# SwiGLU by seven block products in place of eight, in a two-layer decoder trunk

## The chip, the cores and the metric

One NeuronCore of a Trainium2 chip runs the whole program. Its engines are TensorE (matmuls and transposes, written PE in the profile, with weight loads as PEld), VectorE (DVE), ScalarE (ACT), GpSimd (POOL) and SyncE (SP, which here only issues transfers). The metric is the time of one execution on the device in microseconds, lower is better. Profile times below are counted from the start of the profiled span.

## The reference: what is computed

Two layers over 512 tokens of width 1024, in float32:

```python
for layer in range(2):
    x = x + 0.5 * swiglu(rmsnorm(x, ffn1_norm[layer]), ffn1_w_gate_up[layer], ffn1_w_down[layer])
    x = x + hybrid_mixer(rmsnorm(x, mix_norm[layer]), ...)     # 8 forgetting heads, 4 differential heads
    x = x + 0.5 * swiglu(rmsnorm(x, ffn2_norm[layer]), ffn2_w_gate_up[layer], ffn2_w_down[layer])
return rmsnorm(x, final_norm)

def swiglu(h, w_gate_up, w_down):                              # 1024 -> 2 x 2816 -> 1024
    g, u = split(h @ w_gate_up, 2)
    return (silu(g) * u) @ w_down
```

So there are four SwiGLU blocks and two mixers. The change concerns the SwiGLU blocks and the form in which x is kept between all of them.

## The kernel before, in words

Each float32 operand of a matmul is split into two parts of the engine's reduced type, hi and lo, and a product is three matmuls: hi·hi, hi·lo, lo·hi (`mm3`, L341 to L346). Weights are streamed: SP loads a raw block of 128x1024 into one of three buffers, ScalarE copies it to hi (L65), VectorE subtracts to lo (L66); `ensure` and `next_w` (L92, L98) keep two blocks ahead of use.

x is kept with features on partitions, as eight tiles of 128 features x 512 tokens (`xT`). Weights are the stationary operand and x, or the hidden tile, is the moving one, 512 columns wide. `ffn` (L349) runs in three phases of 8, 7 and 7 tiles of 128 hidden features. For each such tile, 24 matmuls make the gate and 24 the up product in two PSUM banks; VectorE multiplies both by the tokens' reciprocal root mean square (L377, L380), ScalarE applies SiLU (L378), VectorE multiplies (L381), and the result is split into hh and hl (L384, L385). At the end of a phase eight down products, one for each 128 output features, are added to x by VectorE (L398). After the last phase `norm_tile` (L187) makes the gained hi and lo of the x tile for what follows (L183, L184) and its squares (L168), which VectorE adds up (L175); `norm_finish` (L199) sums them over partitions with two matmuls.

The last block's last down product is done the other way round, with tokens on partitions (`last_down`, L263), for which x is transposed (`x_tokens`, L220); the final norm follows token tile by token tile.

The mixer (L403) projects, runs attention by head with a schedule that spreads projection matmuls between score steps, and ends with an output projection over eight tiles of output features (`out_part`, L786). The order in which each engine takes its instructions is fixed when the program is built: a planner of the framework takes the program's order as priority, and places each instruction by its dependences and its own estimates of durations. At run time each engine takes its queue in that order, and an instruction that has to wait holds up those behind it on the engine; SP's transfers likewise.

Of the kernel before, what the change touches and what calls it, by code (L numbers as in the profile page):

```python
# [8 lines left out]
F32 = mybir.dt.float32  # L9
# [9 lines left out]
KT = D // P  # L19
FF = 2816  # L20
FT = FF // P
# [5 lines left out]
QKB = 4  # L27
HELD = 4
WARM = 10
A_BANKS = 3  # L30
# [13 lines left out]
def trunk(ctx, tc, x, gains, gain_row, w_gu, w_dn, w_dl, w_in, w_ff, w_out, fbias, lams, subln, consts, rope, out):  # L44
# [5 lines left out]
    wp = ctx.enter_context(tc.tile_pool(name="wp", bufs=3))  # L50
    tp = ctx.enter_context(tc.tile_pool(name="tp", bufs=2))
# [4 lines left out]
    def psum(tag):  # L56
        return ps.tile([P, S], F32, tag=tag, name=f"ps_{tag}", bufs=A_BANKS if tag == "a" else 8 - A_BANKS)

    # ---------------------------------------------------------------- weight stream
    def load_w(src, cols):  # L60
        raw = wp.tile([P, 1024], F32, tag="raw", name="raw")
        hi = wp.tile([P, 1024], F32R, tag="whi", name="whi")
        lw = wp.tile([P, 1024], F32R, tag="wlo", name="wlo")
        sp.dma_start(out=raw[:, :cols], in_=src)
        act.copy(out=hi[:, :cols], in_=raw[:, :cols])  # L65
        dve.tensor_tensor(out=lw[:, :cols], in0=raw[:, :cols], in1=rf(hi[:, :cols]), op=ALU.subtract)  # L66
        return hi, lw

    stream = []
    for l in range(DEPTH):  # L70
        for j in range(2):
            n = 2 * l + j
            if j == 1:
                for b in range(24):
                    stream.append((w_in[l, b], 1024))
                for d in range(KT):
                    if d != 3:
                        stream.append((w_out[l, d], 1024))
            for ph, (f0, f1) in enumerate(PHASES):
                for f in range(f0, f1):  # L80
                    stream.append((w_gu[n, f, 0], 1024))
                    stream.append((w_gu[n, f, 1], 1024))
                if n == 2 * DEPTH - 1 and ph == len(PHASES) - 1:
                    for f in range(f1 - f0 - HELD):
                        stream.append((w_dl[f], 1024))
                    continue
                for d in range(KT):
                    stream.append((w_dn[n, d, :, f0 * P:f1 * P], (f1 - f0) * P))
    ready = []
    pos = [0]  # L90

    def ensure(n):  # L92
        while len(ready) < n and pos[0] < len(stream):
            src, cols = stream[pos[0]]
            pos[0] += 1
            ready.append(load_w(src, cols))

    def next_w(ahead=2):  # L98
        ensure(1 + ahead)
        return ready.pop(0)  # L100

    # ---------------------------------------------------------------- first loads
    gains_sb = const.tile([P, 7, KT], F32, name="gains_sb")
    warm_in = const.tile([P, 5], BF16, name="warm_in")
# [4 lines left out]
    # the clock of the tensor engine comes up while the first loads are on their way, and so does ScalarE's table  # L109
    act.activation(out=zero, in_=zero, func=AF.Silu)  # L110
    warm_ps = psum("b")
    for i in range(WARM):
        pe.matmul(warm_ps[0:1, :], warm_in[:, 0:1], warm_in[:, 0:1].broadcast_to([P, S]) , start=True, stop=True)
    xT = [sb.tile([P, S], F32, tag=f"x{d}", name=f"x{d}") for d in range(KT)]
    # x and the first two blocks of weights, in the order of their use
    sp.dma_start(out=xT[0], in_=x[:, 0, :])
    first_w = [[wp.tile([P, 1024], dt_, tag=tag, name=tag) for tag, dt_ in (("raw", F32), ("whi", F32R), ("wlo", F32R))]
               for _ in range(2)]

    def first_dma(half):  # L120
        cs = slice(half * S, half * S + S)
        for c in range(2):
            sp.dma_start(out=first_w[c][0][:, cs], in_=stream[c][0][:, cs])

    def first_split(half):
        cs = slice(half * S, half * S + S)
        for raw, hi, lo in first_w:
            act.copy(out=hi[:, cs], in_=raw[:, cs])  # L128
            dve.tensor_tensor(out=lo[:, cs], in0=raw[:, cs], in1=rf(hi[:, cs]), op=ALU.subtract)  # L129

    first_dma(0)
    for d in range(1, KT):
        sp.dma_start(out=xT[d], in_=x[:, d, :])
        if d == 2:
            first_dma(1)
    ready.extend([(hi, lo) for _, hi, lo in first_w])
    pos[0] = 2

    def first_consts():
        sp.dma_start(out=ident, in_=consts[:, 0:P])  # L140
        stage = sb.tile([P, 2 * S], F32, tag="vf0", name="stage")
        sp.dma_start(out=stage[:, 0:3 * P], in_=consts[:, P:4 * P])
        pool.tensor_copy(out=ones, in_=stage[:, 2 * P:3 * P])
        pool.tensor_copy(out=identb, in_=ident)
        pool.memset(maskw[:, 0:S - P], 0.0)
        pool.tensor_copy(out=maskb, in_=stage[:, 0:P])
        pool.memset(eps_t, EPS)
        pool.dma_start(out=subln_sb, in_=subln)
        pool.dma_start(out=fb_sb, in_=fbias.partition_broadcast(P))
        for j in range(2):  # L150
            pool.memset(rf(pt3[j][:, 0:P]), 0.0)
# [12 lines left out]
    nstate = {}  # L164

    def square_tile(d):
        sq = tp.tile([P, S], F32, tag="t", name="sq", bufs=6)
        act.activation(out=sq, in_=xT[d], func=AF.Square)  # L168
        if d == 0:
            nstate["acc"] = tp.tile([P, S], F32, tag="acc", name="acc", bufs=1)  # L170
            nstate["sq0"] = sq
        elif d == 1:
            dve.tensor_tensor(out=nstate["acc"], in0=nstate["sq0"], in1=sq, op=ALU.add)
        else:
            dve.tensor_tensor(out=nstate["acc"], in0=nstate["acc"], in1=sq, op=ALU.add)  # L175

    def gain_tile(n, d):
        if d == 0:
            nstate["xg"] = []
        g = gains_sb[:, n, d:d + 1]  # L180
        hi = sb.tile([P, S], F32R, tag=f"xh{d}", name=f"xh{d}")
        lo = sb.tile([P, S], F32R, tag=f"xl{d}", name=f"xl{d}")
        act.activation(out=hi, in_=xT[d], func=AF.Copy, scale=g)  # L183
        dve.scalar_tensor_tensor(out=lo, in0=xT[d], scalar=g, in1=rf(hi), op0=ALU.mult, op1=ALU.subtract)  # L184
        nstate["xg"].append((hi, lo))

    def norm_tile(n, d):  # L187
        """x tile d is final: its gained hi/lo parts and its squares."""
        gain_tile(n, d)
        square_tile(d)  # L190
# [8 lines left out]
    def norm_finish(tag):  # L199
        acc = nstate["acc"]  # L200
        ah = tp.tile([P, S], F32R, tag="pth", name="acch", bufs=3)
        al = tp.tile([P, S], F32R, tag="ptl", name="accl", bufs=3)
        act.copy(out=ah, in_=acc)
        dve.tensor_tensor(out=al, in0=acc, in1=rf(ah), op=ALU.subtract)
        p = psum(tag)
        pe.matmul(p, ones, ah, start=True, stop=False)
        pe.matmul(p, ones, al, start=False, stop=True)
        v = tp.tile([P, S], F32, tag="t", name="v", bufs=6)
        dve.tensor_scalar(out=v, in0=p, scalar1=1.0 / D, scalar2=EPS, op0=ALU.mult, op1=ALU.add)
        rb = tp.tile([P, S], F32, tag="rb", name="rb", bufs=1)  # L210
        act.activation(out=rb, in_=p, func=AF.Sqrt, scale=1.0 / D, bias=eps_t)
        dve.reciprocal(out=rb, in_=rb)
        t = tp.tile([P, S], F32, tag="t", name="tn", bufs=6)
        refine(rb, v, t)
        return rb

    # ---------------------------------------------------------------- the end, with tokens on partitions
    xt, held = [], []

    def x_tokens(t):  # L220
# [738 lines left out]
```

## Time and profile before

| | |
|---|---|
| median of 3 runs | 1956.35 us (1955.96 to 1957.78) |
| profiled execution, span from first to last instruction | 1950.8 us |
| TensorE busy | 1935.1 us, 99% |
| VectorE busy | 1067.3 us, 55% |
| ScalarE busy | 789.9 us, 40% |
| read from HBM | 183.12 MB |
| mean granted TensorE clock | 0.999 |

The page gives the profiled execution's span; its time outside the span isn't listed. A share of busy time is a mean over stages that differ, so it is to be read by stage. Matmuls are pipelined: a duration of 389 ns in a row is not the distance to the next one, which is read from start times. For VectorE both are of use: how long an instruction takes, and how soon the next one may start.

### The profile page before, as it was taken

The numbers are of one execution on the slowest core, as the hardware profiler recorded it, in microseconds if no ns is written. First come the engines' busy times: TensorE is split into PE (matmuls) and PEld (weight loads), VectorE is DVE, ScalarE is ACT, GpSimd is POOL, SyncE is SP. The second block draws the span as 40 slices with busy tenths as digits, with TensorE's granted clock in tenths as the row PEclk, the third lists the DMA queues.
The fourth block names the chain that finished last, engine by engine and source line by source line (L and its number), as shares of the span: only waits on it lengthen the run. The fifth ranks groups of instructions, "written<-read, shape, count | busy, mean of one in ns | idle before, by whom it ended". The sixth has DMA issues, their size and how long they took to land.

```text
span 1950.8 us, 22643 instructions
## 1 busy us (share of the span) xinstructions
PE 1935.1 (99%) x8798; PEld 1585.9 (81%) x8798; DVE 1067.3 (55%) x1750; ACT 789.9 (40%) x1279; POOL 18.6 (1%) x25
## 2 busy tenths in 40 slices
PE   9999999999999999999999999999999999999998
PEld 6888887888878888888888888878788888888886
DVE  7434444678687544434564344456787874344453
ACT  5223223467794322222432232234677842222242
POOL 1000000000000000000000000000000000000002
PEclk9999999999999999999999999999999999999999
DMA  5322333344332232332323223233433233322331
GB/s 179 98 97 95 89 102 104 99 137 120 98 98 97 97 98 98 89 105 94 101 93 100 92 96 97 97 108 119 116 109 114 88 113 97 98 97 88 103 123 44
DMA packets 65179, 199.34 MB, mean 102 GB/s; under 512 B 9096, under 2 KB 9608, under 8 KB 65072
## 3 DMA queue, kind: packets, MB, share of 16 engines
q1 hardware_dynamic: 63424, 195.94, 31.8%
q10 hardware_dynamic: 1584, 1.93, 0.3%
q8 instruction: 69, 1.13, 0.2%
q14 instruction: 38, 0.31, 0.0%
q0 software_dynamic: 64, 0.03, 0.0%
HBM read 183.12 MB, written 2.16 MB: 95 GB/s over the span
## 4 chain that ended last, share of the span: by engine, by line
PE 95%; DMA 2%; DVE 1%; ACT 1%; issue 0%; SPq 0%; ACTq 0%; DVEq 0%
PE ps_a L344 16%; PE ps_a L345 16%; PE ps_a L346 16%; PE ps_b L346 12%; PE ps_b L344 12%; PE ps_b L345 12%; PE ps_b L663 1%; PE ps_a L456 1%; PE ps_a L457 1%; PE ps_a L458 1%; PE ps_b L612 1%; PE ps_b L613 1%; DMA lt<-lams 1%; PE ps_b L704 1%; PE ps_b L705 0%
## 5 line engine op out<-in xcount | busy, mean ns | idle before, releaser
L65 ACT CAST whi<-raw 128x1024 fp32r<-128x1024 f32 (+1 forms) x327 | 338.0, 1034 | 934.9 <-PE ps_a L345 408.1
L66 DVE TENSOR_TENSOR wlo<-raw,whi 128x1024 fp32r<-128x1024 f32 (+1 forms) x327 | 392.3, 1200 | 50.5 <-ACT whi L65 45.1
L344 PE MATMUL ps_a<-xh,whi 128*128 128x512 f32 x960 | 378.9, 395 | 1.0 <-ACT whi L128 0.5
L345 PE MATMUL ps_a<-xl,whi 128*128 128x512 f32 x960 | 374.4, 390 | 0.7 <-DVE xl L184 0.6
L346 PE MATMUL ps_a<-xh,wlo 128*128 128x512 f32 x960 | 374.6, 390 | 0.0
L344 PE MATMUL ps_b<-xh,whi 128*128 128x512 f32 x704 | 274.1, 389 | 0.2 <-ACT whi L65 0.2
L346 PE MATMUL ps_b<-xh,wlo 128*128 128x512 f32 x704 | 274.0, 389 | 0.0
L345 PE MATMUL ps_b<-xl,whi 128*128 128x512 f32 x704 | 273.9, 389 | 0.0
L344 PEld LDWEIGHTS ps_a<-xh,whi 128*128 128x128 f32 x960 | 180.5, 188 | 38.4 <-ACT whi L128 1.5
L346 PEld LDWEIGHTS ps_a<-xh,wlo 128*128 128x128 f32 x960 | 180.2, 188 | 37.9
L345 PEld LDWEIGHTS ps_a<-xl,whi 128*128 128x128 f32 x960 | 180.4, 188 | 37.1 <-DVE xl L184 1.9
L380 DVE TENSOR_TENSOR u<-ps_b,rb 128x512 f32<-128x512 f32 x88 | 60.8, 691 | 256.1 <-PE ps_b L346 256.1
L377 DVE TENSOR_TENSOR g<-ps_a,rb 128x512 f32<-128x512 f32 x88 | 60.8, 691 | 174.8 <-PE ps_a L346 174.7
L344 PEld LDWEIGHTS ps_b<-xh,whi 128*128 128x128 f32 x704 | 132.1, 188 | 27.9 <-ACT whi L65 0.7
L346 PEld LDWEIGHTS ps_b<-xh,wlo 128*128 128x128 f32 x704 | 132.2, 188 | 27.7 <-DVE wlo L129 0.3
L345 PEld LDWEIGHTS ps_b<-xl,whi 128*128 128x128 f32 x704 | 132.2, 188 | 27.6
L344 PE MATMUL ps_a<-hh,whi 128*128 128x512 f32 x324 | 126.3, 390 | 3.6 <-ACT hh L384 3.6
L345 PE MATMUL ps_a<-hl,whi 128*128 128x512 f32 x324 | 126.3, 390 | 0.4 <-DVE hl L385 0.4
L344 PE MATMUL ps_b<-hh,whi 128*128 128x512 f32 x324 | 126.1, 389 | 0.0
L346 PE MATMUL ps_b<-hh,wlo 128*128 128x512 f32 x324 | 126.1, 389 | 0.0
L345 PE MATMUL ps_b<-hl,whi 128*128 128x512 f32 x324 | 126.1, 389 | 0.0
L346 PE MATMUL ps_a<-hh,wlo 128*128 128x512 f32 x324 | 126.1, 389 | 0.0
(270 smaller groups left out, 2465.2 us busy)
## 6 DMA issues: line engine op xcount, KB each, us to landing
raw<-w_gu SPq DMA_DIRECT2D x174, 512.0 KB, 3.2
raw<-w_dn SPq DMA_DIRECT2D x56, 448.0 KB, 3.3
raw<-w_in SPq DMA_DIRECT2D x48, 512.0 KB, 3.4
raw<-w_dn SPq DMA_DIRECT2D x32, 512.0 KB, 3.5
kdup<-qk_t SPq DMA_DIRECT2D x64, 128.0 KB, 2.3
raw<-w_out SPq DMA_DIRECT2D x16, 512.0 KB, 3.3
qk_c<-qk_b SPq DMA_DIRECT2D x64, 64.0 KB, 2.0
cb<-cum_d SPq DMA_DIRECT2D x16, 256.0 KB, 3.6
```

The costliest lines, as they stand in the source:

```text
L65: act.copy(out=hi[:, :cols], in_=raw[:, :cols])
L66: dve.tensor_tensor(out=lw[:, :cols], in0=raw[:, :cols], in1=rf(hi[:, :cols]), op=ALU.subtract)
L344: pe.matmul(p, lh, rh, start=start, stop=False)
L345: pe.matmul(p, lh, rl, start=False, stop=False)
L346: pe.matmul(p, ll, rh, start=False, stop=stop)
L377: dve.tensor_tensor(out=g, in0=pgu[0], in1=rb, op=ALU.mult)
L380: dve.tensor_tensor(out=u, in0=pgu[1], in1=rb, op=ALU.mult)
L456: pe.matmul(pv[t], xh[:, ts], wh[:, sl], start=k == 0, stop=False)
L457: pe.matmul(pv[t], xh[:, ts], wl[:, sl], start=False, stop=False)
L458: pe.matmul(pv[t], xl[:, ts], wh[:, sl], start=False, stop=k == KT - 1)
L612: pe.matmul(p[:, 0:w], lq, kk[m][:, 0, 0:w], start=True, stop=False)
L613: pe.matmul(p[:, 0:w], lq, kk[m][:, 1, 0:w], start=False, stop=not masked)
```

## The change

Strassen's scheme multiplies two matrices that are cut into 2x2 blocks with seven block products and some sums in place of eight products. Here it is used for both products of every SwiGLU block, in a variant that shares its sums.

- x is kept with tokens on partitions (`xs`, four tiles of 128 tokens x 1024). The left matrix (x, or the hidden tile) is now the stationary operand: blocks of 256 tokens by half of the features. The weights are the moving operand.
- The 2816 hidden features are taken in chunks of 512, 512, 256, 512, 512, 512. For each chunk a gate/up part and, one chunk later, a down part. A part is seven products; each uses one of seven forms of the left matrix (three blocks and four sums, `XFORM`) and one of seven forms of the weights. Three of the weight forms are blocks; four are sums, made by VectorE from raw blocks and partly in place (`five`, `six`, `source`), and then split in hi and lo as before. One split unit of 128x1024 feeds 12 matmuls.
- The split units lie in a ring of five (`RING`), made up to four ahead (`next_w`). Each raw block has its own single buffer (R0 to R2, V0 to V4), loaded when its unit is at most two places away in the stream.
- Results of the products go into PSUM banks that some products share; ScalarE takes three of a part's intermediate results to SBUF, VectorE combines them (five instructions for each of two token tiles, `done` in `gate_up`). Every down product is added to x with its sign by VectorE (`upd` in `down`): 14 per part.
- TensorE transposes x before each norm that follows another stage (`turn_x`) and the hidden tiles before the down part (`turn_h`); ScalarE and VectorE make the seven forms from the transposed tiles and split them (`prep_forms`, `rest`, `form_split`).
- The root mean squares come from ScalarE's accumulated squares with tokens on partitions (`squares`, `rms`). The output projection of the mixer has tokens on partitions too (`out_early`, `out_rest`). The end needs no transposes (`tail`).
- The host lays out the weights in the new block order; the bytes read are the same.

```diff
-PHASES = ((0, 8), (8, 15), (15, 22))
+CHUNKS = (512, 512, 256, 512, 512, 512)
+B11, B21, B22, T1, T2, T3, T4 = range(7)
+XFORM = {"1": B11, "2": B21, "3": B22, "4": T4, "5": T1, "6": T2, "7": T3}
+STEADY = "1562734"
+FIRST = "1256374"
+FINAL = "1267453"
...
-    def load_w(src, cols):
-        raw = wp.tile([P, 1024], F32, tag="raw", name="raw")
...
-        act.copy(out=hi[:, :cols], in_=raw[:, :cols])
-        dve.tensor_tensor(out=lw[:, :cols], in0=raw[:, :cols], in1=rf(hi[:, :cols]), op=ALU.subtract)
+    def split(src, hi, lo):
+        act.copy(out=hi, in_=src)
+        dve.tensor_tensor(out=lo, in0=src, in1=rf(hi), op=ALU.subtract)
+        return hi, lo
...
+    RING = ("G4", "G3", "G2", "G0", "G1")
...
+        def add(out_, a, b):
+            dve.tensor_tensor(out=out_, in0=a, in1=b, op=ALU.add)
+            return out_
...
+                sums["5", h] = add(s, blk("21", h), blk("22", h))
...
+                sums["6", h] = add(s, s5, blk("11", h))
...
+            if f == "3":
+                s = six(h)
+                return add(s, s, blk("12", h))
+            if f == "7":
+                six(h)
+                return add(blk("11", h), blk("11", h), blk("21", h))
+            return blk({"1": "11", "2": "12", "4": "22"}[f], h)
...
+            ready.append((tag, make()))
+            for _, need, _ in stream[pos[0]:pos[0] + 2]:
+                need()
+
+    def next_w(ahead=4, keep=False):
...
+    def product(q, units, per, cols, xf, pp, p_done, unit_done):
...
+        for h in range(units):
+            wh, wl = next_w()
+            for p in range(2):
+                ts = slice(p * P, (p + 1) * P)
+                for i in range(per):
+                    kp = h * per + i
+                    sl = slice(i * cols, (i + 1) * cols)
+                    mm3(pp[p][:, 0:cols], form(xf[kp], f, ts), (wh[:, sl], wl[:, sl]),
+                        start and kp == 0, kp == kps - 1, again)
...
+            def one(kp=kp):
...
+                            pe.transpose(pj[j][:, e * 256 + p * P:e * 256 + (p + 1) * P], hs[j][p][:, o:o + P], ident)
...
+                act.copy(out=b, in_=s1)
...
+                act.copy(out=w[:, 0], in_=s2[:, 1])
+                dve.tensor_tensor(out=w[:, 1], in0=b[:, 0], in1=s2[:, 0], op=ALU.subtract)
+                dve.tensor_tensor(out=w[:, 3], in0=w[:, 0], in1=s2[:, 0], op=ALU.subtract)
+                rest(w, b[:, 1])
...
+        def upd(t, half, src, scale):
+            xc = xs[t][:, half * S:(half + 1) * S]
+            dve.scalar_tensor_tensor(out=xc, in0=src, scalar=scale, in1=xc, op0=ALU.mult, op1=ALU.add)
```

More of the change, by code (lines that the diff above doesn't have):

```diff
@@ L69, in trunk @@
-    stream = []
[L70 to L88, printed above, removed]
+    turn = {}
@@ L112, in trunk @@
     for i in range(WARM):
[L113 to L151, printed above, removed]
+        pe.matmul(warm_ps[0:1, :], warm_in[:, 0:1], warm_in[:, 0:1].broadcast_to([P, S]), start=True, stop=True)
     ident = const.tile([P, P], F32, name="ident")
@@ L197, in refine @@
         dve.tensor_tensor(out=y, in0=y, in1=t, op=ALU.mult)
[L199 to L215, printed above, removed]
@@ L311, in norm_cols @@
-    def norm_cols():
-        p = psum("b")
-        acc = nstate["acc"]
-        for b in range(NB):
-            pe.matmul(p[:, b:b + 1], acc[:, b * P:(b + 1) * P], rf(ones[:, 0:1]), start=True, stop=True)
-        st = sm.tile([P, 2, NB], F32, tag="nst", name="nst", bufs=1)
-        v, t = st[:, 0], st[:, 1]
-        rc = sm.tile([P, NB], F32, tag="rc", name="rc", bufs=1)
-        dve.tensor_scalar(out=v, in0=p[:, 0:NB], scalar1=1.0 / D, scalar2=EPS, op0=ALU.mult, op1=ALU.add)
+    norm = {}
@@ new lines, in squares, with rms @@
+    def squares(half):
+        if half == 0:
+            norm["ss"] = sm.tile([P, NB], F32, tag="ss", name="ss", bufs=2)
+        for t in (2 * half, 2 * half + 1):
+            sq = home("s2", [P, 1024], F32, "sq")
+            act.activation(out=sq, in_=xs[t], func=AF.Square, accum_out=norm["ss"][:, t:t + 1])
+    def rms():
+        st = sm.tile([P, 4, NB], F32, tag="nst", name="nst", bufs=2)
+        v, t, rc, nr = [st[:, i] for i in range(4)]
+        dve.tensor_scalar(out=v, in0=norm["ss"], scalar1=1.0 / D, scalar2=EPS, op0=ALU.mult, op1=ALU.add)
@@ L668, in trans_step @@
             else:
[L669 to L670 removed]
+                th, tl = pair()
                 dst = slice(0, w)
@@ L862, in mixer @@
         run(fill)
[L863 to L883 removed]
+        out_rest()
@@ new lines, in trunk, with ahead, second, a @@
+    held = []
+    def ahead(n):
+        for kp in (2, 3):
+            prep_forms(n, 0, kp)
+        squares(0)
+    def second(n):
+        def a(kps, last):
+            for kp in kps:
+                prep_forms(n, 1, kp)
+            if last:
+                squares(1)
+                rms()
+        return [lambda: a((0, 1), False), lambda: a((2, 3), True)]
+    xf = home("y0", [P, KP, 2, S], F32, "xin")
+    def load_xt(half, kp):
+        hs = slice(half * 256, half * 256 + 256)
+        sp.dma_start(out=xf[:, kp, :, hs], in_=xT[:, kp, :, hs])
@@ new lines, in trunk @@
+    pieces = [first_second]
+    for l in range(DEPTH):
+        n = 3 * l + 1
+        ffn(pieces, to_plain(n, l))
+        for kp in (2, 3):
+            prep_plain(n, 0, kp, held.pop(0))
+        for kp in range(KP):
+            prep_plain(n, 1, kp)
+        squares(1)
+        rms()
+        mixer(l, n + 1)
+        if l < DEPTH - 1:
+            ffn(second(n + 1), to_forms(n + 2))
+            ahead(n + 2)
+            pieces = second(n + 2)
+        else:
+            ffn(second(n + 1), tail)
```

868 lines of the change are left out of this document (565 added, 303 removed).

## The prediction

> **What bounds the kernel now.** I read the page first (span, engine shares, slices, chain), then the table of busy time by stage, then a stretch of one feed-forward block.
>
> ```profile
> span 1950.8 us, 22643 instructions
> PE 1935.1 (99%) x8798; PEld 1585.9 (81%) x8798; DVE 1067.3 (55%) x1750; ACT 789.9 (40%) x1279; POOL 18.6 (1%) x25
> PEclk9999999999999999999999999999999999999999
> PE 95%; DMA 2%; DVE 1%; ACT 1%; issue 0%; SPq 0%; ACTq 0%; DVEq 0%
> ```
>
> TensorE is busy all the time at full granted clock and is 95% of the chain that ended last. VectorE is busy 55%, but that is a mean over unlike stages. By stage (four SwiGLU blocks, two mixers; columns: length, then busy time and instructions of TensorE, weight loads, VectorE, ScalarE, GpSimd):
>
> ```profile
> 20.00:377.00 357.00, 353.79 (x1557) 292.09 (x1558) 172.43 (x207) 109.46 (x135) 1.58 (x1) 1.00 0.31 101
> 377.00:622.00 245.00, 244.51 (x1217) 197.58 (x1216) 185.85 (x450) 169.90 (x357) 0.00 (x0) 1.00 0.37 109
> 622.00:980.00 358.00, 358.00 (x1580) 296.37 (x1580) 171.00 (x202) 108.01 (x132) 0.00 (x0) 1.00 0.31 97
> 980.00:1341.00 361.00, 359.59 (x1585) 297.14 (x1585) 171.89 (x206) 110.02 (x134) 1.52 (x1) 1.00 0.31 99
> 1341.00:1586.00 245.00, 244.78 (x1217) 197.43 (x1216) 186.04 (x449) 170.01 (x357) 0.00 (x0) 1.00 0.37 111
> 1586.00:1951.00 365.00, 357.19 (x1592) 295.60 (x1590) 166.89 (x217) 107.60 (x143) 10.30 (x8) 1.00 0.28 93
> ```
>
> A SwiGLU block takes 358 us (third row) with TensorE full; VectorE works 171 us of it, 48%. So the change cuts the engine that sets the time, and whether that shows depends on what it puts on VectorE. Its real price per instruction is seen in this stretch of VectorE's queue (start, duration, then the idle time before it):
>
> ```profile
> 65.17 0.69 DVE L380 TENSOR_TENSOR u<-ps_b,rb 128x512 f32<-128x512 f32 x1 [3.31 <-PE ps_b L346]
> 65.97 0.69 DVE L381 TENSOR_TENSOR u<-u,g 128x512 f32<-128x512 f32 x1
> 66.58 1.22 DVE L66 TENSOR_TENSOR wlo<-raw,whi 128x1024 fp32r<-128x1024 f32 x1
> 67.72 0.68 DVE L385 TENSOR_TENSOR hl<-u,hh 128x512 fp32r<-128x512 f32 x1
> ...
> 76.05 0.69 DVE L380 TENSOR_TENSOR u<-ps_b,rb 128x512 f32<-128x512 f32 x1 [3.31 <-PE ps_b L346]
> ```
>
> The step repeats after 10.88 us (65.17 to 76.05), and it holds 48 matmuls of 512 columns: 0.2267 us each. On VectorE an instruction of 512 columns lasts 0.69 us but the next may start after 0.61 (65.97 to 66.58); one of 1024 lasts 1.22 and hands over after 1.14 (66.58 to 67.72). An instruction that needs the result of the one in front of it starts 0.80 us behind it (65.17 to 65.97). So each VectorE instruction has two prices, pace and full duration. Rows for the shapes that the change uses:
>
> ```profile
> L66 DVE TENSOR_TENSOR wlo<-raw,whi 128x1024 fp32r<-128x1024 f32 x271 | 331.1, 1222 | 44.7 <-ACT whi L65 44.3
> L65 ACT CAST whi<-raw 128x1024 fp32r<-128x1024 f32 x271 | 285.0, 1052 | 763.6 <-PE ps_a L345 353.2 <-issue 297.5 <-PE ps_b L345 109.4
> L398 DVE SCALAR_TENSOR_TENSOR x<-ps_a,x 128x512 f32<-128x512 f32 x44 | 30.4, 692 | 102.1 <-PE ps_a L346 102.1
> L674 DVE TENSOR_TENSOR ptl<-ps_b,pth 128x256 fp32r<-128x256 f32 x24 | 9.9, 414 | 1.9 <-ACT pth L673 1.9
> L488 DVE SCALAR_TENSOR_TENSOR vf<-ps_a,rc,vf 128x256 fp32r<-128x256 f32 x12 | 5.2, 479 | 1.6 <-ACT vf L486 1.6
> ```
>
> Between 512 and 1024 columns both prices rise by 0.53 us; from that slope I estimate a pace of 0.345 us for 256 columns, 0.875 for 768, 1.405 for 1280 (full: 0.414 by the row, 0.96, 1.49).
>
> **TensorE, per block.** Removed: 22 x 48 matmuls of gate and up and 528 of down, 1584 in all. Added: each of the five 512-wide chunks takes 7 products x 24 = 168 matmuls of 512 columns in gate/up and 84 in down; the 256-wide one takes 168 of 256 columns and 42 of 512. That makes 1302 wide and 168 narrow ones. Both narrow matmuls and transposes have rows from elsewhere in the trace:
>
> ```profile
> 426.73 0.28 PE L612 MATMUL ps_b<-kk,q 128*128 128x256 f32 x1
> ...
> 427.20 0.40 PE L344 MATMUL ps_a<-xh,whi 128*128 128x512 f32 x1
> ```
>
> ```profile
> 1836.13 0.87 PE ps_b L232 x8
> ```
>
> Four narrow ones stand between 426.73 and 427.20: 0.118 us each; a transpose is 0.109. The block: 1302 x 0.2267 + 168 x 0.118 = 315.0; the 88 transposes that bring the hidden tile from token rows to feature rows 9.6; the 32 that turn x 3.5. Sum 328.1 against 358: 30 us less per block if TensorE still set the time.
>
> **VectorE, per block** (pace / full duration). A weight unit of 128x1024 now feeds 12 matmuls (2.72 us of TensorE), not 24, and four of seven units are sums that VectorE must first add.
> - Weights: a 512 chunk has 14 splits and 8 sums for gate/up, 7 and 4 for down: 33; the 256 chunk 11 of 1024 and 11 of 512. So 176 wide ones and 11 half ones: 207.3 / 222.7.
> - Gate and up out of PSUM: 10 instructions per chunk, 50 of 512 and 10 of 256: 34.0 / 38.7.
> - Hidden tiles into their seven forms, 11 pairs of feature tiles, each four of 256, one of 512, one of 1280: 3.40 / 3.84, so 37.4 / 42.2.
> - Down products into x, 14 per chunk (two for each product) where there were 24 per block: 84 of 512: 51.2 / 58.1.
> - x into forms: four pairs, each two of 512, four of 256 (0.48 with a per-token or gain scalar, by L488), one of 768: 13.9 / 17.0. Norm scalars: some ten tiny ones, 1.6 / 1.8.
>
> The sum is 345 at pace, 380 at full durations. ScalarE copies 112 whole weight units at 1.05 us and 7 halves (some 122 us), evicts, and makes and splits the forms: I estimate 205 of 358 us, not a bound. So **VectorE, not TensorE, sets the block's length after the change**: 345 > 328 even if it never waits. Neither end is likely alone: independent neighbours hand over at pace, while a sum, its ScalarE copy and its subtraction are a chain, and evictions wait for TensorE in a queue whose order is fixed. I take the middle, 362 us (VectorE idle or held for 5% of the block), 4 us more than now. Four blocks: +16 (bounds -52 and +88).
>
> The Trainium skill, VectorE: DVE Perf Modes, section on the DRAIN, says that the next instruction does not start until the pipe of the one before has emptied, and that leaving waits out does not avoid it. By that the upper end, 380, would be the sum; the rows above, 1.14 against 1.22, show earlier starts for independent neighbours, so the trace doesn't bear it out for those.
>
> **What is hidden or moved.** The adds of squares and the wide reciprocal of the norm leave VectorE; in the mixer TensorE is full (244.5 of 245), so they are worth nothing there. The mixer keeps its matmuls and nearly all else: 0. The raw bytes stay the same; the transfers:
>
> ```profile
> raw<-w_gu SPq DMA_DIRECT2D x174, 512.0 KB, 3.2
> ```
>
> Raw tiles have one buffer each, so a load on SP's queue waits for the subtraction that last read its tile, and the loads queued behind it wait too. A ring of five split units gives TensorE 13.6 us of lead, so I take 0 here; without that cover see below.
>
> **Joints.** At a block's end VectorE runs out of weights to make while TensorE eats the ring: between 0 and one ring (13.6 us); with VectorE the bound the ring is nearly empty, so 3 us x 4 = 12. Before a mixer, the last update of x (0.69), a group of transposes (0.44), the gained pair (estimated at 0.9, twice L488's 0.48) stand between two matmuls: 2 us x 2 = 4; now the projection takes x tile by tile. Start and end:
>
> ```profile
> 5.85 0.50 PE L344 MATMUL ps_a<-xh,whi 128*128 128x512 f32 x1 [0.53 <-ACT whi L128]
> ```
>
> ```profile
> 1943.22 0.69 DVE L289 SCALAR_TENSOR_TENSOR xt<-ps_b,xt 128x512 f32<-128x512 f32 x1 [0.95 <-PE ps_b L346]
> ```
>
> The first real matmul comes at 5.85; after the change a whole 1024-column block and a form made in two steps stand ahead of it: 0 to 6, I take 3. At the end one tile of tokens takes from 1943.2 to the span's end, 7.6 us; now two tiles end together and their chains partly overlap: 0 to 4, I take 2.
>
> **Sum.** 1950.8 + 16 + 12 + 4 + 3 + 2 = 1987.8 us span. The median of the runs shown, 1956.35, lies 5.55 above the profiled span (launch and end outside it); kept, the time is 1993.
>
> **The rivals.**
> - *VectorE runs without a gap* (faster). Place: the steady chunks of each block; price: 345 in place of 362, and no loss at the joints of the ring. Time 1950.8 - 52 + 9 + 5.5 = 1913. For it: the planner knows that work is plentiful, five units of ring smooth it, and TensorE's stalls cost nothing then. Against: a chunk needs 57.1 + 1.8 us of TensorE and 59 of VectorE, so two full engines wait for each other's results with little slack. It decides once VectorE is over 97% busy in a block: below 358 us. Chance 0.28.
> - *TensorE still sets the time*: 1950.8 - 120 + 9 + 5.5 = 1846. It would need VectorE's work to be 17 us per block cheaper than its own pace; for it only that I may misjudge a shape. 0.05.
> - *Full durations*: most VectorE instructions are held by the one before (sums in place, copy, subtraction). 380 per block: 1993 + 72 = 2065. For it: 0.80 between dependent neighbours; against it, much else is ready. 0.18.
> - *Loads late*: at a down part's end (four times a block another gate/up part follows) the second product needs a tile freed by the last subtraction. If nothing hides issue and landing, some 4 us x 16 = 64: 2057. For it: the loads of six tiles crowd into four units; against it, 3.2 us per load and the ring's lead. 0.06.
> - *Break-even*: 358 per block, within 0.2%. 0.07.
>
> **How the numbers follow.** The forecast, 1993, has 0.36; its own range is 1965 to 2040. What a measurement can tell here is about 0.2%, 4 us. Faster: 0.28 + 0.05 = 0.33. Same: 0.07. Slower: 0.36 + 0.18 + 0.06 = 0.60. The range for 8 in 10 runs from just under the gapless case to above the late loads and the full durations: 1905 to 2085.
>
> **What would show it.** Right: VectorE at 90 to 97% in the four blocks, TensorE at about 328 busy of some 366 with waits named VectorE's weight subtraction, the chain with a large VectorE share, the mixers at 245. If VectorE is busy over 97% and a block is under 358 us, the gapless rival holds; if TensorE is 99% busy, my VectorE count is wrong; if VectorE's idle time is put down to transfers into raw tiles, the loads were late. Wrong altogether: a wide matmul that is not 0.227 us with tokens stationary, or a longer mixer.

## The result, and the profile after

The changed kernel takes 1969.98 us (median of 4 runs, 1962.3 to 1971.61), the kernel before 1956.15 us beside it. The ratio is 1.0066, 95% interval 1.0045 to 1.0086: slower, by 14 us. The forecast was 37 us slower. That its sign came out is luck: the SwiGLU blocks, which were to lose the time, came out slightly faster, and the mixers, which it put at nothing, lost more than that. The profiled execution took 1969.73 us, with a span of 1967.9.

From the page of the kernel after: the span, the busy times, the granted clock in 40 slices, the chain of work that ended last.

```profile
span 1967.9 us, 24074 instructions
PE 1866.3 (95%) x8798; PEld 1513.3 (77%) x8798; DVE 1765.7 (90%) x2675; ACT 1138.9 (58%) x1800; POOL 8.8 (0%) x20
PEclk8999999999999999999999999989999999999998
PE 62%; DVE 21%; ACT 9%; DMA 4%; issue 3%; SPq 0%; ACTq 0%; DVEq 0%
```

VectorE went from 1067 to 1766 us busy, and TensorE's share of the chain fell from 95% to 62%. To see where the time went, the stages are cut at the first matmul of each. The table of busy time by stage of the kernel before, in the order block 1, mixer 1, blocks 2 and 3, mixer 2, block 4 (columns: bounds, length, then busy time and instructions of TensorE, weight loads, VectorE, ScalarE and GpSimd, the granted clock, the transfer engines' share, GB/s):

```profile
5.85:372.82 366.97, 362.45 (x1586) 297.22 (x1587) 182.19 (x222) 118.97 (x150) 4.49 (x4) 1.00 0.33 108
372.82:615.71 242.89, 242.40 (x1207) 195.82 (x1206) 185.16 (x449) 168.45 (x355) 0.00 (x0) 1.00 0.37 109
615.71:975.29 359.58, 359.58 (x1588) 297.67 (x1587) 171.26 (x202) 108.84 (x132) 0.00 (x0) 1.00 0.31 97
975.29:1336.81 361.52, 360.11 (x1587) 297.59 (x1586) 172.32 (x206) 110.64 (x135) 1.52 (x1) 1.00 0.31 99
1336.81:1579.74 242.93, 242.71 (x1207) 195.72 (x1206) 185.35 (x448) 168.58 (x355) 0.00 (x0) 1.00 0.37 112
1579.74:1950.80 371.06, 363.44 (x1619) 300.80 (x1617) 170.76 (x222) 111.22 (x147) 10.30 (x8) 1.00 0.28 93
```

The same table of the kernel after, in an order of its own: blocks 2, 3, 1, 4, then the two mixers.

```profile
631.85:985.00 353.15, 336.18 (x1586) 276.46 (x1584) 341.70 (x431) 192.38 (x254) 0.00 (x0) 0.99 0.29 99
984.98:1346.16 361.18, 345.24 (x1616) 282.72 (x1614) 350.42 (x447) 198.76 (x269) 0.62 (x1) 0.98 0.27 95
8.98:375.33 366.35, 343.38 (x1590) 279.88 (x1591) 352.63 (x448) 202.51 (x273) 1.74 (x4) 0.97 0.32 111
1603.40:1967.90 364.50, 336.46 (x1575) 276.37 (x1573) 348.94 (x457) 196.38 (x268) 5.05 (x4) 0.97 0.27 91
375.33:631.85 256.52, 249.69 (x1214) 197.73 (x1215) 185.25 (x448) 171.85 (x366) 0.00 (x0) 0.99 0.35 109
1346.16:1603.40 257.24, 251.36 (x1215) 199.03 (x1216) 185.40 (x447) 171.65 (x366) 0.00 (x0) 0.99 0.35 109
```

The four blocks sum to 1459.1 us before and 1445.2 after: 14 us shorter. The two mixers sum to 485.8 and 513.8: 28 us longer. The first matmul comes at 8.98 us, not 5.85: 3 us. So the kernel is slower because of its mixers, whose mathematics the change leaves alone, and the blocks came out slightly ahead. (The two profiled spans differ by 17 us, which is 28 and 3 less 14; the medians differ by 14, since the profiled execution before was faster than the runs in its median.) In the blocks VectorE is busy 95.7 to 97.0% of the time; TensorE's busy time there is 340 us on average, more than the 328 us of work that the prediction counted, since matmuls behind a wait or at a lowered clock last longer (rows in the last section). The waits of the kernel after (engine, what waited, for what: us in total, times, longest):

```profile
ACT wg L82 <- DVE fs L111: 201.8, 60, 10.5
...
ACT wg L82 <- DMA raw<-w_gu: 18.7, 14, 3.0
...
PE ps_c L366 <- DVE wg L83: 16.1, 16, 1.4
PE ps_c L365 <- DVE x L494: 15.9, 10, 2.4
```

ScalarE waits 202 us for VectorE's weight sums (`fs`, line 111) and 19 us for loads of gate/up weights. TensorE waits for VectorE in two ways: for the low half of a split weight (`wg`, line 83), and for a down product to be added into x (line 494), which frees its PSUM bank (a bank is one of the result memory's parts into which matmuls write). VectorE's own work, by shape (busy, mean ns of one, idle time before):

```profile
L83 DVE TENSOR_TENSOR wg<-raw,wg 128x1024 fp32r<-128x1024 f32 x312 | 377.0, 1222 | 37.7 <-ACT wg L82 36.8
L83 DVE TENSOR_TENSOR wg<-fs,wg 128x1024 fp32r<-128x1024 f32 x192 | 234.9, 1225 | 18.6 <-ACT wg L82 17.8
L111 DVE TENSOR_TENSOR fs<-fs,raw 128x1024 f32<-128x1024 f32 x128 | 156.2, 1221 | 0.1
L494 DVE SCALAR_TENSOR_TENSOR x<-ps_c,x 128x512 f32<-128x512 f32 x192 | 124.9, 687 | 3.0 <-PE ps_c L367 2.9
...
L83 DVE TENSOR_TENSOR hf<-hb,hf 128x512 fp32r<-128x512 f32 x44 | 30.3, 688 | 0.0
```

### The profile page after: what moved, and what is told of

Same layout as the page of the kernel before. It is cut to its first block, busy times and chain, and to the rows that moved or that the text cites. A ratio compares the mean times of both kernels' runs of the same rounds, so it can differ in the third digit from the quotient of the medians.

```text
span 1967.9 us, 24074 instructions
## 1 busy us (share of the span) xinstructions
PE 1866.3 (95%) x8798; PEld 1513.3 (77%) x8798; DVE 1765.7 (90%) x2675; ACT 1138.9 (58%) x1800; POOL 8.8 (0%) x20
## 4 chain that ended last, share of the span: by engine, by line
PE 62%; DVE 21%; ACT 9%; DMA 4%; issue 3%; SPq 0%; ACTq 0%; DVEq 0%
PE ps_c L366 10%; PE ps_c L367 10%; PE ps_c L365 9%; DVE wg L83 7%; PE ps L366 6%; PE ps L367 6%; PE ps L365 5%; ACT wg L82 3%; PE ps_a L365 2%; DVE hf L83 2%; PE ps_a L366 2%; PE ps_a L367 2%; DVE fs L111 2%; DMA raw<-w_gu 2%; DVE x L494 2%
## 5 line engine op out<-in xcount | busy, mean ns | idle before, releaser
L82 ACT CAST wg<-raw 128x1024 fp32r<-128x1024 f32 (+1 forms) x328 | 336.3, 1033 | 303.7 <-PE ps L367 76.5
L83 DVE TENSOR_TENSOR wg<-raw,wg 128x1024 fp32r<-128x1024 f32 (+1 forms) x328 | 388.0, 1196 | 37.7 <-ACT wg L82 36.8
L82 ACT CAST wg<-fs 128x1024 fp32r<-128x1024 f32 (+1 forms) x204 | 208.9, 1027 | 194.7 <-DVE fs L111 180.8
L366 PE MATMUL ps_c<-wg,xf 128*128 128x512 f32 (+1 forms) x768 | 290.2, 378 | 16.2 <-DVE wg L83 16.1
L365 PE MATMUL ps_c<-wg,xf 128*128 128x512 f32 (+1 forms) x768 | 285.9, 380 | 9.5 <-ACT wg L82 8.4
L367 PE MATMUL ps_c<-wg,xf 128*128 128x512 f32 (+1 forms) x768 | 287.6, 375 | 0.0
L83 DVE TENSOR_TENSOR wg<-fs,wg 128x1024 fp32r<-128x1024 f32 (+1 forms) x204 | 243.1, 1193 | 18.6 <-ACT wg L82 17.8
L366 PE MATMUL ps<-wg,xf 128*128 128x512 f32 (+1 forms) x576 | 217.3, 377 | 7.1 <-DVE wg L83 7.1
L365 PE MATMUL ps<-wg,xf 128*128 128x512 f32 (+1 forms) x576 | 215.6, 378 | 7.5 <-ACT wg L82 7.0
L367 PE MATMUL ps<-wg,xf 128*128 128x512 f32 (+1 forms) x576 | 215.6, 375 | 0.4 <-DVE xf L83 0.4
L366 PEld LDWEIGHTS ps_c<-wg,xf 128*128 128x128 f32 x768 | 146.0, 190 | 49.7 <-DVE wg L83 24.5
L365 PEld LDWEIGHTS ps_c<-wg,xf 128*128 128x128 f32 x768 | 145.5, 190 | 39.1 <-ACT wg L82 12.7
L367 PEld LDWEIGHTS ps_c<-wg,xf 128*128 128x128 f32 x768 | 145.9, 190 | 24.9
L111 DVE TENSOR_TENSOR fs<-fs,raw 128x1024 f32<-128x1024 f32 (+1 forms) x136 | 161.7, 1190 | 0.1
L365 PE MATMUL ps_c<-wg,hf 128*128 128x512 f32 x352 | 142.3, 404 | 16.0 <-DVE x L494 15.9
L366 PE MATMUL ps_c<-wg,hf 128*128 128x512 f32 x352 | 140.5, 399 | 0.0
L367 PE MATMUL ps_c<-wg,hf 128*128 128x512 f32 x352 | 139.7, 399 | 0.0
L366 PEld LDWEIGHTS ps<-wg,xf 128*128 128x128 f32 x576 | 109.6, 190 | 29.4 <-DVE wg L83 11.2
L365 PEld LDWEIGHTS ps<-wg,xf 128*128 128x128 f32 x576 | 108.9, 190 | 27.5 <-ACT wg L82 8.4
L367 PEld LDWEIGHTS ps<-wg,xf 128*128 128x128 f32 x576 | 109.5, 190 | 20.1 <-DVE xf L83 1.3
## 6 DMA issues: line engine op xcount, KB each, us to landing
raw<-w_dn SPq DMA_DIRECT2D x16, 256.0 KB, 3.7
rope<-cum_d SPq DMA_DIRECT2D x16, 256.0 KB, 4.3
```

Source lines behind the costliest of these rows:

```text
L82: act.copy(out=hi, in_=src)
L83: dve.tensor_tensor(out=lo, in0=src, in1=rf(hi), op=ALU.subtract)
L111: dve.tensor_tensor(out=out_, in0=a, in1=b, op=ALU.add)
L365: pe.matmul(p, lh, rh, start=start, stop=False, skip_group_check=again)
L366: pe.matmul(p, lh, rl, start=False, stop=False, skip_group_check=again)
L367: pe.matmul(p, ll, rh, start=False, stop=stop, skip_group_check=again)
```

## The experiments

Theory A: the blocks last as long as VectorE's work, at pace, with some 4% between its instructions. Theory B: they lose their time on TensorE's own side (turns, transposes, the lowered clock). Theory C concerns GpSimd, which is idle: work moved there slows VectorE.

**Leave the weight sums out.** All products, splits and transposes stay; the four summed weight forms are replaced by one of their raw blocks, so the output is another.

```diff
         def add(out_, a, b):
-            dve.tensor_tensor(out=out_, in0=a, in1=b, op=ALU.add)
-            return out_
+            return a
```

> The VectorE additions that make four of the seven weight forms are left out (a form that is a sum is replaced by one of its blocks, so the result is not the reference's); matmuls, copies and subtractions stay. Theory A (VectorE sets the length of the SwiGLU blocks after the change): 64 additions of some 1.14 us less per block, VectorE falls from about 345 to 272 us busy, TensorE takes over at about 330 us per block, and the run is some 80 to 100 us shorter: 1870 to 1890. Theory B (the blocks are held by TensorE, its stalls at joints and its clock, and VectorE's load is only high): within 15 us of 1970. The mixers stay at 257 us in both.

It took 1861.8 us in its one execution (span 1860.0), faster than the 1870 to 1890 of theory A. Blocks 2 and 3 of this kernel by stage:

```profile
602.72:932.69 329.97, 329.60 (x1592) 276.48 (x1590) 275.61 (x367) 197.28 (x257) 0.00 (x0) 1.00 0.32 104
932.69:1266.41 333.72, 331.69 (x1610) 278.45 (x1608) 277.41 (x377) 199.84 (x267) 1.58 (x1) 1.00 0.32 103
```

With 66 to 73 us less on VectorE a block takes 330 and 334 us and TensorE is full at full clock. That is TensorE's own price for the seven products with their transposes (the turns), 328 by the prediction's sum; the lowered clock adds nothing once VectorE keeps up. Its mixers (254.4 and 253.2 us) stay long.

**Leave a third of TensorE's block work out.** The low-by-high matmul of each product is dropped in the SwiGLU blocks.

```diff
         pe.matmul(p, lh, rh, start=start, stop=False, skip_group_check=again)
+        if two:
+            pe.matmul(p, lh, rl, start=False, stop=stop, skip_group_check=again)
+            return
         pe.matmul(p, lh, rl, start=False, stop=False, skip_group_check=again)
```

> In the SwiGLU blocks the third of the three matmuls of each product (lo by hi) is left out, so the result is less exact; VectorE's and ScalarE's work is unchanged. TensorE has a third less to do in a block: about 105 us of 328. Theory A (VectorE sets the blocks' length): blocks stay at 345 us or more, the run at 1930 to 1970. Theory B (TensorE sets it): blocks fall towards 250, the run towards 1560.

It took 2003.42 us in its one execution: a third less work for TensorE in the blocks, and 33 us more, which is also above theory A's 1930 to 1970. Blocks 2 and 3:

```profile
640.24:999.58 359.34, 281.57 (x1087) 205.51 (x1086) 338.94 (x427) 190.09 (x251) 0.00 (x0) 0.88 0.30 97
999.58:1373.02 373.44, 283.97 (x1132) 204.31 (x1131) 352.66 (x447) 199.96 (x271) 0.61 (x1) 0.90 0.29 92
```

VectorE's work is the same, 339 and 353 us, and the blocks are longer than with all matmuls. So B is out. The granted clock in these blocks is 0.88 and 0.90, against 0.98 to 0.99; that slower single matmuls, with more idle time between them, make VectorE wait longer for its inputs is a likely reason for the extra 6 and 12 us, but no run here isolates it.

**Move the sums to GpSimd**, all of them (shown below), or only those for products 5 and 7, by an argument of `add` at these two places.

```diff
-            dve.tensor_tensor(out=out_, in0=a, in1=b, op=ALU.add)
+            pool.tensor_tensor(out=out_, in0=a, in1=b, op=ALU.add)
```

> All weight sums go from VectorE to GpSimd, nothing else changes. GpSimd's row before shows 1.29 us for 512 columns, so some 2.4 us for 1024: 155 us per block, within its time. Theory A: VectorE's load falls as in the run without sums, blocks towards 330 to 340 us, the run to 1880 to 1920. Rival C: GpSimd's additions slow VectorE's instructions or come too late in their chain of sum, copy and subtraction (a sum of 2.4 us where a unit is used up in 2.7): no gain, 1960 or above.

> Half of the weight sums, those of forms 5 and 7, go to GpSimd; 6 and 3 stay on VectorE. Theory A: 32 x 1.14 = 36 us less VectorE work per block, about 309, below TensorE's 328: blocks 332 to 342, the run 1885 to 1925, near the run with all sums moved. Rival C: as there, half as bad, 1960 to 1990.

All on GpSimd: 2128.89 us, ratio 1.0892 (1.0876 to 1.0908) to the kernel before. Half: 2025.13 us, ratio 1.0364 (1.0345 to 1.0382), slower than the 1960 to 1990 of rival C too. VectorE's rows with all sums on GpSimd, to be held against the five rows of the kernel after above:

```profile
L83 DVE TENSOR_TENSOR wg<-raw,wg 128x1024 fp32r<-128x1024 f32 x312 | 469.7, 1515 | 55.7 <-ACT wg L82 54.7 <-DMA raw<-w_dn 0.4
L83 DVE TENSOR_TENSOR wg<-fs,wg 128x1024 fp32r<-128x1024 f32 x192 | 318.6, 1668 | 89.0 <-ACT wg L82 88.8
L494 DVE SCALAR_TENSOR_TENSOR x<-ps_c,x 128x512 f32<-128x512 f32 x192 | 124.1, 680 | 6.1 <-PE ps_c L367 5.9
...
L83 DVE TENSOR_TENSOR hf<-hb,hf 128x512 fp32r<-128x512 f32 x44 | 71.8, 1633 | 0.0
```

And GpSimd's own:

```profile
L111 POOL TENSOR_TENSOR fs<-fs,raw 128x1024 f32<-128x1024 f32 x128 | 366.4, 2866 | 223.6 <-DVE wg L83 181.5 <-issue 22.6 <-ACT xf L82 13.9
```

An add takes GpSimd 2.87 us where VectorE took 1.22, and while it runs VectorE's subtractions grow from 1.22 to 1.52 and 1.67 us, its 512-wide one from 0.69 to 1.63. The update of x, which reads one operand from PSUM, stays at 0.68. Theory C holds, and it costs more than the sums did. VectorE executes the same 2403 instructions here as in the run without sums, but is busy 1818.3 us in place of 1482.6, 336 us more; making the sums itself had cost it 283 (1765.7 in the kernel after). Its idle time grew as well, from 202 to 310 us: VectorE waited 18.6 us before the subtractions of summed forms, nearly all for ScalarE's copies, and now waits 89.0, so sums that come late have a part in the loss, and the runs do not separate the two parts. The Trainium skill, SBUF — State Buffer, section "Who interferes with whom", says that a VectorE instruction with two SBUF inputs contends with a GpSimd instruction that reads SBUF, over a port pair that it calls an exclusive lock, while one with at most one SBUF input, outside the 2-port modes, does not contend. The rows agree on which instructions are slowed and which are not.

**Eight products in the down parts.** If VectorE binds, give TensorE back some matmuls. An eighth product saves the four weight sums, three splits, the forms of the hidden tile and six of 14 updates of a down part, by my estimate some 17 us of VectorE per chunk of 512 for 2.7 us of TensorE. First in chunks 0 to 4, then in 0, 2 and 4 only, as shown.

```diff
+PLAIN = (0, 2, 4)
...
+    def down_plain(c, after, yf):
+        for half in range(2):
+            pp = [banks("b", "ps_c"), banks("a", "ps_5")]
+            for e in range(2):
+                wh, wl = next_w()
+                for t in range(2):
+                    for p in range(2):
+                        for kp in range(kps):
...
+                            mm3(pp[t][p], form(yf[kp], 2 * t + e, slice(p * P, (p + 1) * P)), (wh[:, sl], wl[:, sl]),
+                                e == 0 and kp == 0, e == 1 and kp == kps - 1)
```

> The down products of chunks 0 to 4 of every SwiGLU block are done as eight block products on the four weight blocks themselves; only chunk 5 keeps seven there, and gate/up keeps seven throughout. Per chunk of 512 that adds 12 wide matmuls (2.7 us at 0.2267) on TensorE and takes from VectorE 4 sums and 3 subtractions of 1024 (8.0 us at 1.14) and the forms and updates that go with seven products, about 17 us in all. Theory A (VectorE's time binds the blocks): TensorE 340 us a block, VectorE about 268, so TensorE binds again and a block takes 342 to 348; 1890 to 1915 us in all. Theory B (the blocks lose their time on TensorE's own side, by turns and lowered clock, not by VectorE): twelve more us of matmuls a block, and the time is 1985 to 2015 us.

> The same, in chunks 0, 2 and 4 alone. TensorE 335 us a block, VectorE about 302. Theory A: the surplus of VectorE in one chunk is made good in the next if four to five units of lead bridge it: a block 338 to 345, 1875 to 1900 us in all, the fastest of the splits. If the lead doesn't bridge it, chunks 1 and 3 run at VectorE's 63 us and the others at TensorE's 62: 1895 to 1915. Theory B: 1975 to 1995.

1934.24 us, ratio 0.9894 (0.9877 to 0.9910), and 1926.36 us, ratio 0.9854 (0.9839 to 0.9869). Both beat both kernels, which is theory A's sign against B's, but both miss its ranges, by 19 and 26 us. Of the second kernel the stretch from the third part of block 2 on, and a wait from TensorE's timeline:

```profile
709.88:901.00 191.12, 191.12 (x952) 162.33 (x951) 173.62 (x205) 95.02 (x122) 0.00 (x0) 1.00 0.29 94
```

```profile
367.87 0.79 PE L380 MATMUL ps_a<-XA,wg 128*128 128x512 f32 x1 [6.11 <-ACT wg L83]
```

In the steady part TensorE is busy 191.12 of 191.12 us, in the chunks with seven products too: a surplus of VectorE in one chunk is made good in the next. So the miss lies outside the steady part. 6.1 us before each mixer were of this edit's own making: with fewer units a block ends at another place of the ring of five, and the tile that the mixer wants first is the one that TensorE is still reading. The rest was not traced; the mixers, still long (256.0 us the first), and the blocks' first parts are where I had counted little.

**The mixers.** Before the change four w_out tiles were split by the end of attention, now seven. The same 30 us near the end of attention in the first mixer, kernel before, then after (TensorE, weight loads, VectorE, ScalarE, GpSimd, clock):

```profile
557.00:587.00 30.00, 30.00 (x176) 24.14 (x175) 23.92 (x76) 27.50 (x73) 0.00 (x0) 1.00 0.24 71
```

```profile
560.00:590.00 30.00, 27.07 (x143) 20.39 (x144) 24.95 (x77) 29.20 (x75) 0.00 (x0) 0.94 0.32 93
```

ScalarE went from 92% to 97% and TensorE is no longer full. TensorE's longest waits in the whole first mixer, kernel after (7.0 us in all), then its only one in the kernel before:

```profile
PE ps_b L890 <- ACT pair L860: 1.9, 3, 0.9
PE ps_a L365 <- ACT XA L319: 1.3, 2, 0.9
```

```profile
PE ps_b L612 <- DVE ptl L674: 0.4, 1, 0.4
```

Two edits of the kernel after, each alone: the high parts of the w_out tiles copied by GpSimd (`gp` is set for these tiles only), and the turns of x at the mixer's end spread over the products of the second half.

```diff
-        act.copy(out=hi, in_=src)
+        if gp:
+            pool.tensor_copy(out=hi, in_=src)
+        else:
+            act.copy(out=hi, in_=src)
```

> The change as it stands, with the high parts of the w_out tiles (7 copies of 128x1024 per mixer, on ScalarE before) on GpSimd. Theory M1 (the mixer is longer because ScalarE is full at the end of attention, 98, 95 and 99% from 560 to 590 us, with three more w_out tiles split there than before the change): the waits for pair and pg go, each mixer 4 to 8 us shorter, 1955 to 1962 us. Rival M2 (GpSimd's copies lengthen VectorE's instructions beside them, or come later themselves): no shorter, 1968 to 1980.

```diff
             for k in (4, 5, 6, 7):
                 for g in GR2:
                     out_mm(po2[g], g, 1, k, k == 4, False)
-            for kp in range(KP):
-                prep_forms(n_next, 0, kp)
+                prep_forms(n_next, 0, k - 4)
```

> The change as it stands, with the turns of x's first half at the mixer's end put one behind each k of the second half's products in place of all four behind the last of the four. No matmul more or less. Theory M3 (ScalarE and VectorE sit idle 8 to 10 us for turns that stand late in TensorE's queue, and the block behind pays for it): mixer and joint 2 to 5 us shorter each, 1960 to 1966 us. Rival: TensorE never waits for those forms, the time is the same within 2 us.

With the copies on GpSimd: 1956.76 us, ratio 1.0006 (0.9996 to 1.0016), inside the expected range, and the loss of 14 us against the kernel before is gone. Its two mixers:

```profile
377.37:629.00 251.63, 247.98 (x1214) 197.69 (x1215) 185.10 (x448) 165.43 (x359) 9.19 (x7) 0.99 0.37 112
1342.94:1593.50 250.56, 247.46 (x1215) 197.65 (x1215) 184.74 (x447) 165.53 (x359) 9.33 (x7) 0.99 0.37 112
```

They are 4.9 and 6.7 us shorter, 11.6 of the 28. A copy takes GpSimd 1.04 us, but four of the 14 took 1.8 to 2.1, and a few of VectorE's instructions beside them grew. One such case, in the second mixer, first VectorE's rows, then GpSimd's:

```profile
1520.94 1.21 DVE L86 TENSOR_TENSOR XA<-raw,XA 128x1024 fp32r<-128x1024 f32 x1
...
1522.31 1.28 DVE L754 TENSOR_TENSOR qk<-kdup,qk 128x512 fp32r<-128x512 f32 x1 [0.16 <-ACT qk L753]
```

```profile
1520.98 2.07 POOL L83 CAST XA<-raw 128x1024 fp32r<-128x1024 f32 x1 [1.74 <-DVE pair L864]
```

The copy began beside a subtraction and took twice its time; VectorE's next instruction with two SBUF inputs, 0.69 us elsewhere, lasted 1.28, past the copy's end. It happens too seldom to show in the sum: VectorE is busy 185 us in the mixer as before. Spreading the turns gave 1970.53 us, ratio 1.0077 (1.0061 to 1.0092): nothing, as its rival said. ScalarE and VectorE do sit idle for those turns, but TensorE never waits for what they then make.

**Together**, with the mixer's ring entered where the block leaves it: eight products in chunks 1 and 3, or in 0, 2 and 4, both with the copies on GpSimd. The lines are the second's; the first has the order G0, G1, G2.

```diff
-    MIX = ("G1", "G2", "G0")
+    MIX = ("G2", "G0", "G1")
```

> Eight products in the down parts of chunks 1 and 3 alone, the ring of weight tiles entered by the mixer one place earlier (the order G0, G1, G2 in place of G1, G2, G0, since the block now ends one place elsewhere in the ring), and the high parts of the w_out tiles on GpSimd. TensorE 333.5 us a block, VectorE about 311. From 1926 us with chunks 0, 2 and 4: less 12.2 (two waits of 6.1 for the mixer's first weight tile, which that kernel's ring order made), less 10 to 13 (the w_out copies), less 5 (12 wide matmuls fewer in two of the blocks' chunks, net): 1896 to 1904 us if a lead of five units carries VectorE over chunks 4 and 5. Rival: it doesn't, VectorE binds there as it did over the whole block before, 2 to 4 us a block are lost and the time is 1904 to 1916.

> The same with chunks 0, 2 and 4, and the mixer's ring order G2, G0, G1. TensorE 335 us a block, VectorE about 302, so more slack and 5 us more matmuls in all: 1901 to 1908 us if TensorE binds everywhere. If the wait for the mixer's first weight tile stays (the new order frees that tile two units before the block's end, not four), 1908 to 1918.

Chunks 1 and 3: 1921.8 us, ratio 0.9836 (0.9823 to 0.9850), slower than its expected range and than its rival's, 1904 to 1916. Chunks 0, 2 and 4: **1900.95 us, ratio 0.9724 (0.9711 to 0.9737)**, just under its expected range and 54 us less than the kernel before beside it (1954.66). Of this kernel, by stage: block 2, mixers 1 and 2, and the steady stretch inside block 2:

```profile
610.77:952.83 342.06, 338.15 (x1621) 283.15 (x1620) 308.09 (x376) 182.24 (x238) 0.00 (x0) 1.00 0.31 102
...
361.24:610.77 249.53, 246.52 (x1215) 196.48 (x1215) 185.64 (x449) 165.12 (x358) 8.38 (x7) 1.00 0.39 112
1297.37:1545.07 247.70, 245.80 (x1214) 196.53 (x1215) 185.19 (x448) 165.14 (x358) 9.14 (x7) 1.00 0.38 113
675.00:908.00 233.00, 233.00 (x1137) 197.10 (x1137) 204.72 (x239) 116.55 (x146) 0.00 (x0) 1.00 0.35 115
```

The 6.1 us waits are gone and TensorE is busy 233 of 233 us, with VectorE at 88%. The variant with chunks 1 and 3 has less TensorE work and yet loses 21 us to it. Part of the reason is that its last two chunks both use seven products. The end of block 2, from the last gate/up part's end on, first with chunks 1 and 3, then with 0, 2 and 4 (this row starts 0.4 us before that point):

```profile
915.08:961.96 46.88, 42.46 (x201) 34.42 (x200) 46.17 (x64) 23.62 (x34) 0.00 (x0) 1.00 0.24 79
```

```profile
908.00:952.83 44.83, 44.83 (x215) 37.11 (x214) 41.86 (x57) 22.25 (x32) 0.00 (x0) 1.00 0.19 61
```

VectorE is at 46.17 of 46.88 us there and TensorE idles 4.4; with a plain chunk 4 TensorE is full. Blocks 2 and 3 are 4.0 and 6.5 us longer, where the rival had said 2 to 4; their ends, from the first matmul of the last down part on, hold 2.4 and 3.8 us of that, and the rest of the 21 us was not traced.

## Why the prediction was wrong in size, by its steps

- **TensorE, 328.1 us a block.** Right. Without the sums, when nothing else binds, blocks 2 and 3 take 330.0 and 333.7.
- **VectorE, 345 us at pace, 380 at full durations, and the bound.** Right as a count and as a mechanism: 341.7 to 352.6 us busy, mean 348.4, and the blocks follow VectorE's work and not TensorE's. No block is near 380. The sentence on the DRAIN that the prediction cited is qualified in the same section, "The DRAIN you can't avoid", of the Trainium skill, VectorE: DVE Perf Modes: a next op that is not held starts earlier. The rows shown there, 1.14 against 1.22 us, agree.
- **The middle, 362 us, with 3 us of joint at each end.** This term was mis-sized. By its own terms the prediction had 4 x 362 + 18 = 1466 us for the blocks with their joints and the end; they took 1445.2, with VectorE idle 3.6% of them, all edges included. It shows best in block 2, 365 us by these terms and 353.2 measured. Pace was the nearer end; that the ring and independent work let VectorE run on is a likely reason, not tested by itself. At block 2's end TensorE did not eat an emptying ring as the step on joints says: it waited 2.41 and 2.06 us for updates of x, each of which frees a bank (rows in the last section).
- **The difference to before.** This step failed too, and worse. The 362 were set against 358, a stretch without edges, and the edges were then added to the new kernel alone. The blocks before, cut at first matmuls, sum to 1459.1, not 4 x 358 = 1432. That is 27 us of wrong baseline, 9 and 13 of it in blocks 1 and 4, which hold the start and the end. With the 21 us of the step above it turns +34 into -14.
- **"The mixer keeps its matmuls and nearly all else: 0."** This failed, and it made the sign: +13.6 and +14.3 us. I had looked at TensorE's full 244.5 of 245 us and not at ScalarE, which near the end of attention had no room for three more w_out splits of 1.05 us. Taking the copies of all seven off ScalarE returned 11.6 of the 28 us. Another 2 us per mixer are the 16 transposes of x that now stand in its end (2.3 us busy), work that the prediction counted in the block. For the remaining 5 to 7 per mixer the trace has small waits, for the first tiles of x at its start and on ScalarE for probabilities in attention, and TensorE at half clock: one spell of some 3.4 us in the first mixer and two in the second, 1.7 us of work lost in each, where the kernel before had none. They were not tried one by one, so this part of the cause stays open.
- **Before a mixer, 2 us each.** Block 3, which ends at a mixer, is 8.0 us longer than block 2, where before it was 1.9. But the pieces that the step named are small there: in the last 16 us TensorE waits 0.6 us for an update of x and 0.5 us for the first gained tile. VectorE has 8.7 us more to do in block 3 (350.4 against 341.7), and with VectorE the bound that would count in full; TensorE's clock is also lower in it (0.98 against 0.99). No run separates the two.
- **Start, 3 us.** Right: 3.1.
- **What lies outside the span, 5.55 us.** Wrong: the profiled execution after has 1.8 us outside it. So have the later runs of the kernel before (1.7 to 1.8). The 5.55 mixed a faster profiled execution of that kernel with the median of others. That is 3.7 us.
- **Loads late.** It did not happen: ScalarE waits 18.7 us in all for gate/up loads and 11.3 for those of the down parts.

The terms meet the measured time, as differences of the two profiles must: 1993.35 less 48 for the blocks, plus 28 for the mixers, less 3.7 outside the span is 1969.7, the time of the profiled execution. Of the rivals, the gapless one came closest in the blocks (block 2 took 353 us, under its mark of 358, with VectorE at 96.8%, just short of its 97%), and its 1913 would have needed unchanged mixers as well as VectorE idle 1.6% of the blocks in place of 3.6%.

## What to carry to other kernels

A saving on one engine is worth only what the next one leaves, and the best split of those tried is a mixture: seven products in the gate/up parts, seven and eight by turns in the down parts, within the reach of the buffers, made 1970 into 1901 us here, together with some copies moved to an idle engine. Cut before and after at the same events when lengths are subtracted; a steady stretch is not a baseline. A stage that keeps its arithmetic can still pay if another engine gets the same work earlier: look at every engine of the stage over 90% in the stretch into which something moves.

## What the runs showed of the hardware that was not expected

TensorE's clock fell to half after short waits. The end of block 2 on TensorE's timeline in the kernel after (start, duration, idle time before it):

```profile
965.37 0.50 PE L365 MATMUL ps<-wg,hf 128*128 128x512 f32 x1 [2.41 <-DVE x L494]
...
969.08 0.47 PE L365 MATMUL ps_c<-wg,hf 128*128 128x512 f32 x1 [2.06 <-DVE x L494]
969.39 0.40 PE L366 MATMUL ps_c<-wg,hf 128*128 128x512 f32 x1
...
970.73 0.63 PE L365 MATMUL ps_c<-wg,hf 128*128 128x512 f32 x1
971.15 0.63 PE L366 MATMUL ps_c<-wg,hf 128*128 128x512 f32 x1
```

Two waits of 2.41 and 2.06 us, six matmuls between them, and from 970.3 on a matmul is 0.42 us from the next (970.73 to 971.15), not 0.227; the granted clock from 970.3 to 973.5 is 0.50, and the spell ends after about 3.4 us. The Trainium skill, TensorE: Matmul & The Clock Gate, section "HAM oscillation — how this bites in real kernels", gives the rule of no idle gaps over about 3.4 us; here each gap is shorter. In the blocks the lowered clock is a follower, not the cause: where the waits went (without the sums, or with the mixture) the granted clock is back at 1.00 in the blocks.

Also not expected: removing a third of TensorE's work made its stage longer, and GpSimd's additions cost VectorE more than making them itself, though 14 copies by GpSimd in the mixers met its instructions so seldom that its busy time there did not grow.
